# Attention scores: the queries' low part on half the rows, and one maximum per component

## The chip, the cores and the metric

The kernel runs on one core of a Trainium2 chip. The metric is device time in microseconds (us): the time of one execution, as the median of several. Names used below: PE is TensorE (matrix products), PEld its weight loads, DVE is VectorE, ACT is ScalarE, POOL is GpSimd, SP is the engine whose queue issues the loads and stores. PSUM is the memory that products are written to; it is divided into banks of 512 float32 columns.

## The reference

The layer takes 1024 latent tokens and 256 context tokens of width 1024. One projection feeds two branches, a gated linear attention and a differential attention; gates merge them, and an output projection follows. The change lies in the differential attention. It has 8 heads, and each head has two components with 64 channels:

```python
# k1, k2: 256 context keys and 1024 latent keys; q1, q2: 1024 latent queries
s1 = jnp.einsum('bhqd,bhkd->bhqk', qb1, k1).astype(jnp.float32) * scale
s2 = jnp.einsum('bhqd,bhkd->bhqk', qb2, k2).astype(jnp.float32) * scale
a = jax.nn.softmax(s1, axis=-1) - lam * jax.nn.softmax(s2, axis=-1)
return jnp.einsum('bhqk,bhkv->bhqv', a.astype(v.dtype), v)
```

Queries and keys are normalised and rotated before this. All inputs and the output are float32.

## The kernel before

**Numbers in two parts.** TensorE works on a faster float32 format of reduced precision (`fp32r` in the rows of the profile). A value is therefore split into a high and a low part, x = hi + lo, and a product of two values is made as several products of parts, summed in PSUM. For the large projections these are three (`mm3`, L331): hi x hi, hi x lo, lo x hi.

**Three phases.** Phase A makes the projections and the linear attention and stores queries, keys and values to device memory (DRAM). Phase B, about 938 to 1468 us in the profile, is the differential attention. Phase C makes the remaining branch projections and the output projection.

**Scores.** A unit is one head and 128 queries: 64 units in all. A score product contracts 64 channels, while the array has 128 rows. The rows are used for the keys' two parts: `att_keys` (L1379) loads, for each component, a tile `kk` of 128 rows and 1280 columns with the keys' high part in rows 0 to 63 and their low part in rows 64 to 127. `att_queries` (L1398) loads, for each component and each pair of query blocks, a tile `aq` with the queries' high and low part (second index 0 and 1), the same in both halves of the rows. One product with the queries' high part as weights so gives qhi x (khi + klo), and a second one with their low part adds qlo x (khi + klo). `score` in `att_scores` (L1430) issues these two for each piece of columns.

**Pieces and banks.** The scores of a unit fill five PSUM banks, the tile `s5` with 2560 columns: component 0 in columns 0 to 1279, component 1 in 1280 to 2559. Bank 2 holds the end of component 0 and the beginning of component 1, 256 columns each (`TAIL`); the other banks hold two pieces of 512 columns per component (`MAIN`). A unit has 12 products: 8 with 512 columns, 4 with 256. Three counters guard the banks: `s0` and `s1` for a component's main pieces, `st` for the shared bank. A component's counter is free again after its exponential, `st` after both.

**Softmax.** `att_max` takes a negated maximum on VectorE: one over 1024 columns for each component, and one over the shared bank for both. `att_exp` joins a component's two values with a minimum (`tensor_scalar`) and then makes the exponential of all 1280 columns on ScalarE, with the row sum as a by-product. `att_mix` joins the two components on VectorE. Then TensorE transposes the result (`att_tr`), ScalarE and GpSimd split it into parts (`split2`), and TensorE multiplies it with the values (`att_av`).

**What sets the order.** All instructions except loads and stores are put in an order by a planner (`Driver`, L57), before the program runs: tasks are generators, and each runs when what it waits for is ready by the planner's own costs (`mm` at L325 for products, `Engine` for the others); among those due, the lowest priority number goes first. On the chip each engine works through its list in that order. `yield AtPE(0)` inside a task lets other tasks place products in between. `acq` and `rel` take and give back buffers at planned times. `fill` has the last priority: its projections (24 products of 512 columns per half tile) go wherever TensorE would be free in phase B. What is left of it goes to phase C. All loads and stores go through SP's queue. `banked` (L336) declares which engine's work shares a bank with which, so that only these wait for one another.

Of the kernel before, what the change touches and what calls it, by code (L numbers as in the profile page):

```python
# [12 lines left out]
AF = mybir.ActivationFunctionType  # L13
ALU = mybir.AluOpType
AX = mybir.AxisListType
# [206 lines left out]
class Hybrid:  # L222
# [99 lines left out]
            yield  # L322
        self.d.spawn(later(), AtPE(at), prio=-9)

    def mm(self, out, lhsT, rhs, start, stop, more=False):  # L325
        self.ins = self.nc.tensor.matmul(out, lhsT, rhs, start=start, stop=stop, skip_group_check=more).ins  # L326
        n = rhs.free_size()
        c = 0.009 + max(n, 230) * 0.000428 if rhs.dtype == F32R else 0.006 + max(4 * n, 470) / 2400
        return self.d.op("PE", c, [out], [lhsT, rhs])

    def mm3(self, out, sh, sl, mh, ml, first, last, more=False):  # L331
# [1047 lines left out]
    def att_keys(self):  # L1379

        for hd in range(8):
            c, x = hd // 4, hd % 4
            for i in range(10):
                yield self.ev_st["dk", c, i]
            if hd:
                yield self.ev_q[0, 1]
            K = []
            for comp in range(2):
                rows = slice(64 * comp, 64 * comp + 64)
                yield from self.acq("kk")  # L1390
                kt = self.t("kk", [P, T], F32R)
                self.dma(kt[0:64], self.d_kT[0][c][x, rows])
                self.dma(kt[64:128], self.d_kT[1][c][x, rows])
                K.append(kt)
            self.K[hd] = K
            self.d.set(self.ev_k[hd], self.d.when(*K))

    def att_queries(self):  # L1398
        yield self.ev_b2
        for hd in range(8):  # L1400
            c, x = hd // 4, hd % 4
            for pr in range(4):
# [3 lines left out]
                for comp in range(2):  # L1406

                    src = self.d_qT[c][x, 64 * comp:64 * comp + 64, :, pr * 256:(pr + 1) * 256]
                    yield from self.acq("aq")
                    qt = self.t("aq", [P, 2, 256], F32R)  # L1410
                    for hh in range(2):
                        self.dma(qt[64 * hh:64 * hh + 64], src)
                    Q.append(qt)
                self.Q[hd, pr] = Q
                self.d.set(self.ev_q[hd, pr], self.d.when(*Q))
# [14 lines left out]
    def att_scores(self):  # L1430
# [4 lines left out]
        for hd in range(8):  # L1435
            for qt in range(8):
# [2 lines left out]
                yield self.ev_q[hd, pr]  # L1439
                K, Q = self.K[hd], self.Q[hd, pr]  # L1440

                def score(po, comp, o, n):
                    bank = po.offset % (2 * T) // 512
                    for j in range(2):
                        e = self.mm(po, Q[comp][:, j, qs], K[comp][:, o:o + n], j == 0, j == 1)
                        self.banked(self.ins, "PE", bank)
                    return e

                u = dict(hd=hd, qt=qt, E=[None, None], mt=self.t("sm", [P, 2]), mx=[self.t("sm", [P, 1]) for _ in range(2)],
                         z=self.t("sm", [P, 2]), left=2, ev=[Event() for _ in range(3)])  # L1450

                for comp in range(2):
                    yield from self.acq(f"s{comp}")
                    pm = s5[:, 1536 * comp:1536 * comp + 1024]
                    for x, (o, n) in enumerate(self.MAIN[comp]):
                        e = score(pm[:, x * 512:(x + 1) * 512], comp, o, n)
                        if x == 0:
                            yield AtPE(0)
                    d.spawn(self.att_max(u["ev"][comp], u["mx"][comp], pm, 3 * comp, 3 * comp + 1), On(e, "DVE"), prio=-3)
                    yield AtPE(0)  # L1460
                    if comp == 0:
                        yield from self.acq("st")
                        pt = s5[:, 1024:1536].rearrange("p (c k) -> p c k", c=2)
                        for x in range(2):
                            e = score(pt[:, x], x, *self.TAIL[x])
                        d.spawn(self.att_max(u["ev"][2], u["mt"], pt, 2), On(e, "DVE"), prio=-3)
                    elif qt == 7:
                        self.rel("kk", e, 2)
                    d.spawn(self.att_exp(u, comp, s5), On(e, "DVE"), prio=-3)
                    yield AtPE(0)  # L1470
                if qt % 2 == 1:
                    self.rel("aq", e, 2)
                d.set(self.ev_u[8 * hd + qt])

    def att_max(self, ev, mx, pm, *banks):
        self.dve.tensor_reduce(mx, pm, AX.X, ALU.max, negate=True)
        self.banked(self.dve.ins, "DVE", *banks)
        self.d.set(ev)
        return
        yield  # L1480

    def att_exp(self, u, comp, s5):
        d, mx = self.d, u["mx"][comp]
        yield u["ev"][2]
        yield u["ev"][comp]
        yield d.on("DVE", mx)
        self.dve.tensor_scalar(mx, mx, u["mt"][:, comp:comp + 1], None, ALU.min)
        yield from self.acq("e5")
        E = u["E"][comp] = self.t("e5", [P, T])
        yield d.on("ACT", mx)  # L1490
        e = self.act.activation(E, s5[:, 1280 * comp:1280 * comp + T], AF.Exp, bias=mx, accum_out=u["z"][:, comp:comp + 1])
        self.banked(self.act.ins, "ACT", *range(2 * comp, 2 * comp + 3))
        self.rel(f"s{comp}", e)
        u["left"] -= 1
        if u["left"] == 0:
# [19 lines left out]
        d.set(self.ev_a[u["hd"], u["qt"]], e)  # L1515


    TAIL = ((1024, 256), (0, 256))
    MAIN = (((0, 512), (512, 512)), ((256, 512), (768, 512)))
    GROUPS = ((0, 4), (4, 4), (8, 2))  # L1520

    def att_tr(self):
# [577 lines left out]
```

## Time and profile before

| | us |
|---|---|
| median of 3 executions | 1720.37 (1717.92 to 1720.63) |
| span of the profiled execution | 1714.5 |
| TensorE busy in it | 1674.2 |
| VectorE busy | 1057.7 |
| ScalarE busy | 738.3 |
| GpSimd busy | 728.8 |
| score products, TensorE busy | 180.5 |

The span runs from the first to the last instruction of one profiled execution; the profile has no other time of that execution, and the times of the other executions include what lies before and after the span. Busy times are not additive: engines work side by side. A row of a timeline gives start, length, engine, line, instruction, "output <- inputs", shape and count, and in brackets the idle time of the engine before it with what ended that. Almost all products have the same line (L326, inside `mm`), so the tiles' names tell them apart: `s<-kk,aq` are scores, `b<-ident,e` transposes, `b<-at,vv` products with the values, `mb<-h,wt` and `mc<-h,wt` projections of `fill`.

### The profile page before, as it was taken

How to read it: one execution, taken by the hardware profiler on the slowest of the kernel's cores; microseconds unless marked ns; L12 is line 12 of the kernel's file. 1: busy time of each engine (PE TensorE's matmuls, PEld its weight loads, DVE VectorE, ACT ScalarE, POOL GpSimd, SP SyncE). 2: the span in 40 equal slices, each digit the busy share in tenths (PEclk: the TensorE clock that was granted, in tenths of full speed). 3: DMA queues.
4: the chain of work that ended last, by engine and by line, in shares of the span. 5: the costliest groups of instructions: out<-in, count | busy, mean ns of one | idle time of the engine just before them, and what ended most of it. 6: DMA issues, size and time to landing. Idle time of an engine off the chain costs nothing.

```text
span 1714.5 us, 24744 instructions
## 1 busy us (share of the span) xinstructions
PE 1674.2 (98%) x8557; PEld 1389.4 (81%) x8557; DVE 1057.7 (62%) x1933; ACT 738.3 (43%) x1509; POOL 728.8 (43%) x917
## 2 busy tenths in 40 slices
PE   8899999999999999999999989999999999999999
PEld 3788788888888888888888878888888888887887
DVE  4534325615564767767763788777877778325694
ACT  4636522212242443344342566656656556311231
POOL 1500002403324445444541577878878778710000
PEclk9999999999999999999999999999999999999999
DMA  8523344453743544535444244435436753269421
GB/s 309 158 86 122 143 154 149 140 171 115 221 163 114 202 142 147 168 125 168 160 129 143 91 119 137 117 108 145 133 105 185 226 156 114 84 238 333 148 98 74
DMA packets 244748, 258.81 MB, mean 151 GB/s; under 512 B 20840, under 2 KB 176400, under 8 KB 244624
## 3 DMA queue, kind: packets, MB, share of 16 engines
q1 hardware_dynamic: 244624, 257.25, 47.7%
q8 instruction: 67, 1.10, 0.3%
q14 instruction: 57, 0.47, 0.1%
HBM read 170.68 MB, written 86.51 MB: 150 GB/s over the span
## 4 chain that ended last, share of the span: by engine, by line
PE 87%; POOL 4%; DVE 2%; DMA 2%; ACT 2%; issue 2%; SPq 0%; ACTq 0%; DVEq 0%; POOLq 0%
PE mm L326 42%; PE mc L326 11%; PE mb L326 8%; PE s L326 7%; PE b L326 5%; POOL at L190 4%; PE b L352 3%; PE go L326 3%; PE gs L326 2%; PE gt L326 2%; PE tp L352 2%; DVE sm L190 1%; PE mz L326 1%; DMA w<-in_w_ada 1%; PE gt L352 1%
## 5 line engine op out<-in xcount | busy, mean ns | idle before, releaser
L326 PE MATMUL mm<-w,h 128*128 128x512 f32 x2304 | 569.3, 399 | 1.5 <-DVE w L190 1.5
L326 PEld LDWEIGHTS mm<-w,h 128*128 128x128 f32 x2304 | 425.6, 188 | 87.6 <-DVE w L190 2.1
L190 POOL TENSOR_TENSOR at<-ac,at 128x512 fp32r<-128x512 f32 (+1 forms) x192 | 239.6, 1248 | 16.0
L190 DVE TENSOR_REDUCE sm<-s 128x1 f32<-128x1024 f32 (+1 forms) x192 | 195.7, 1039 | 55.1 <-PE s L326 47.5
L326 PE MATMUL mb<-h,wt 128*128 128x512 f32 x720 | 200.2, 410 | 1.9 <-DVE ft L190 1.1
L190 ACT ACTIVATE e<-s,sm 128x1280 f32<-128x1280 f32 x128 | 170.0, 1331 | 49.3 <-DVE sm L190 41.5
L326 PE MATMUL s<-kk,aq 128*128 128x512 f32 (+1 forms) x768 | 180.5, 367 | 10.3 <-ACT e L190 3.2
L190 POOL TENSOR_SCALAR at<-ac 128x512 fp32r<-128x512 f32 (+1 forms) x192 | 139.2, 725 | 114.2 <-ACT ac L190 108.8
L190 ACT ACTIVATE ac<-b 128x512 f32<-128x512 f32 (+1 forms) x213 | 106.8, 507 | 141.9 <-PE b L352 103.5
L190 ACT ACTIVATE p<-mm 128x512 f32<-128x512 f32 (+1 forms) x116 | 67.6, 589 | 216.9 <-PE mm L326 198.5
L326 PEld LDWEIGHTS s<-kk,aq 128*128 128x128 f32 x768 | 122.2, 190 | 32.3 <-ACT e L190 12.6
L326 PEld LDWEIGHTS mb<-h,wt 128*128 128x128 f32 x720 | 127.7, 191 | 24.4 <-DVE ft L190 1.8
L326 PE MATMUL mc<-h,wt 128*128 128x512 f32 x624 | 144.1, 390 | 0.8 <-DVE wt L190 0.5
L326 PE MATMUL mm<-h,w 128*128 128x512 f32 x576 | 142.1, 399 | 2.3 <-ACT p L190 1.4
L190 POOL TENSOR_SCALAR sm<-sm 128x1 f32<-128x1 f32 (+1 forms) x78 | 16.8, 216 | 288.6 <-DVE sm L190 166.7
L326 PEld LDWEIGHTS mc<-h,wt 128*128 128x128 f32 x624 | 116.4, 188 | 25.4 <-DVE wt L190 1.0
L326 PE MATMUL b<-at,vv 128*128 128x256 f32 x960 | 132.1, 287 | 0.3
L326 PEld LDWEIGHTS b<-at,vv 128*128 128x128 f32 x960 | 123.5, 192 | 5.2 <-ACT ac L190 1.1
L326 PEld LDWEIGHTS mm<-h,w 128*128 128x128 f32 x576 | 107.1, 189 | 25.4 <-DVE h L190 1.7
L190 DVE TENSOR_TENSOR w<-raw,w 128x512 fp32r<-128x512 f32 x120 | 86.0, 734 | 63.5 <-ACT w L190 62.4
L190 POOL TENSOR_TENSOR sm<-sm,nhalf 128x1 f32<-128x1 f32 (+2 forms) x110 | 109.6, 997 | 10.4 <-DVE sm L190 3.9
L190 DVE SCALAR_TENSOR_TENSOR e<-e,sm,e 128x1280 f32<-128x1280 f32 x64 | 113.3, 1770 | 0.8
(225 smaller groups left out, 2358.6 us busy)
## 6 DMA issues: line engine op xcount, KB each, us to landing
raw<-in_w_in SPq DMA_DIRECT2D x72, 512.0 KB, 4.3
aq<-d_qT SPq DMA_DIRECT2D x128, 128.0 KB, 3.0
d_kT<-pl SPq DMA_DIRECT2D x40, 256.0 KB, 2.3
d_dv<-pl SPq DMA_DIRECT2D x40, 256.0 KB, 2.6
kk<-d_kT SPq DMA_DIRECT2D x32, 320.0 KB, 5.3
gv<-d_v SPq DMA_DIRECT2D x40, 256.0 KB, 2.8
vv<-d_dv SPq DMA_DIRECT2D x16, 640.0 KB, 6.3
d_aT<-gpl SPq DMA_DIRECT2D x64, 128.0 KB, 2.0
```

The lines of the kernel that those rows point to most:

```text
L190: self.ins = f(out, *args, **kw).ins
L326: self.ins = self.nc.tensor.matmul(out, lhsT, rhs, start=start, stop=stop, skip_group_check=more).ins
L352: self.nc.tensor.transpose(out, src, self.ident[:n, :n])
```

## The change

- The queries' low part is multiplied with the keys' high part alone, on 64 rows; the product of the two low parts is no longer computed. A low product uses rows 0 to 63 for the first 1024 columns of component 0, and rows 64 to 127 for the other columns.
- For that, the keys lie differently: in the first 1024 columns of component 0 the high part stays in rows 0 to 63; elsewhere the two parts change places. Component 0's key tile is loaded in four pieces instead of two. Of component 1's query tile the upper half gets the high part only.
- The products of a unit come in another order: the high products of component 0's first two pieces, then a point at which other work may come in between; then, once `s1` and `st` are free, the other four high products and all six low ones without such a point. The low ones change between the halves of the rows: lower 256, upper 512, lower 256, lower 512, upper 512, lower 512 columns.
- In the shared bank the second component's high product no longer starts a sum of its own (`more`); the first component's does.
- The planner counts a low product at half its cost (`half`).
- `att_max` is gone. `att_exp` takes one maximum over all 1280 columns of its component. The maximum over the shared bank and the minima fall away. Both components' softmax tasks are started after the last product of the unit.

```diff
-    def mm(self, out, lhsT, rhs, start, stop, more=False):
+    def mm(self, out, lhsT, rhs, start, stop, more=False, half=False):
...
+        c *= 0.5 if half else 1.0
...
                 kt = self.t("kk", [P, T], F32R)
-                self.dma(kt[0:64], self.d_kT[0][c][x, rows])
-                self.dma(kt[64:128], self.d_kT[1][c][x, rows])
+                for j in range(2):
+                    for c0, n in ((0, T),) if comp else ((0, 1024), (1024, 256)):
+                        o = 64 * (j ^ (comp or c0 > 0))
+                        self.dma(kt[o:o + 64, c0:c0 + n], self.d_kT[j][c][x, rows, c0:c0 + n])
...
                     for hh in range(2):
-                        self.dma(qt[64 * hh:64 * hh + 64], src)
+                        n = 2 if hh >= comp else 1
+                        self.dma(qt[64 * hh:64 * hh + 64, :n], src[:, :n])
...
-                def score(po, comp, o, n):
-                    bank = po.offset % (2 * T) // 512
-                    for j in range(2):
-                        e = self.mm(po, Q[comp][:, j, qs], K[comp][:, o:o + n], j == 0, j == 1)
-                        self.banked(self.ins, "PE", bank)
+                def score(comp, o, lo, more=False):
+                    c0 = 1280 * comp + o
+                    n = 256 if o == self.TAIL[comp] else 512
+                    po = s5[:, c0:c0 + n]
+                    r = slice(0, P) if not lo else slice(0, 64) if c0 < 1024 else slice(64, P)
+                    e = self.mm(po, Q[comp][r, int(lo), qs], K[comp][r, o:o + n], not (lo or more), lo, True, lo)
+                    self.banked(self.ins, "PE", c0 // 512)
                     return e
...
+                yield from self.acq("s0")
+                for o in (0, 512):
+                    score(0, o, False)
+                yield AtPE(0)
+                yield from self.acq("s1")
+                yield from self.acq("st")
+                score(0, 1024, False)
+                score(1, 0, False, True)
+                for o in (256, 768):
+                    score(1, o, False)
+                for comp, o in ((0, 1024), (0, 0), (1, 0), (1, 256), (0, 512), (1, 768)):
+                    e = score(comp, o, True)
+                if qt == 7:
+                    self.rel("kk", e, 2)
                 for comp in range(2):
-                    yield from self.acq(f"s{comp}")
-                    pm = s5[:, 1536 * comp:1536 * comp + 1024]
-                    for x, (o, n) in enumerate(self.MAIN[comp]):
-                        e = score(pm[:, x * 512:(x + 1) * 512], comp, o, n)
-                        if x == 0:
-                            yield AtPE(0)
-                    d.spawn(self.att_max(u["ev"][comp], u["mx"][comp], pm, 3 * comp, 3 * comp + 1), On(e, "DVE"), prio=-3)
-                    yield AtPE(0)
-                    if comp == 0:
-                        yield from self.acq("st")
-                        pt = s5[:, 1024:1536].rearrange("p (c k) -> p c k", c=2)
-                        for x in range(2):
-                            e = score(pt[:, x], x, *self.TAIL[x])
-                        d.spawn(self.att_max(u["ev"][2], u["mt"], pt, 2), On(e, "DVE"), prio=-3)
-                    elif qt == 7:
-                        self.rel("kk", e, 2)
                     d.spawn(self.att_exp(u, comp, s5), On(e, "DVE"), prio=-3)
-                    yield AtPE(0)
+                yield AtPE(0)
...
-    def att_max(self, ev, mx, pm, *banks):
-        self.dve.tensor_reduce(mx, pm, AX.X, ALU.max, negate=True)
+    TAIL = (1024, 0)
+
+    def att_exp(self, u, comp, s5):
+        d = self.d
+        mx = u["mx"][:, comp:comp + 1]
+        sc = s5[:, 1280 * comp:1280 * comp + T]
+        banks = range(2 * comp, 2 * comp + 3)
+        self.dve.tensor_reduce(mx, sc, AX.X, ALU.max, negate=True)
         self.banked(self.dve.ins, "DVE", *banks)
...
-        yield u["ev"][2]
-        yield u["ev"][comp]
-        yield d.on("DVE", mx)
-        self.dve.tensor_scalar(mx, mx, u["mt"][:, comp:comp + 1], None, ALU.min)
         yield from self.acq("e5")
         E = u["E"][comp] = self.t("e5", [P, T])
         yield d.on("ACT", mx)
-        e = self.act.activation(E, s5[:, 1280 * comp:1280 * comp + T], AF.Exp, bias=mx, accum_out=u["z"][:, comp:comp + 1])
-        self.banked(self.act.ins, "ACT", *range(2 * comp, 2 * comp + 3))
+        e = self.act.activation(E, sc, AF.Exp, bias=mx, accum_out=u["z"][:, comp:comp + 1])
+        self.banked(self.act.ins, "ACT", *banks)
         self.rel(f"s{comp}", e)
```

More of the change, by code (lines that the diff above doesn't have):

```diff
@@ L1440, in att_scores @@
                 K, Q = self.K[hd], self.Q[hd, pr]
-                def score(po, comp, o, n):
-                    bank = po.offset % (2 * T) // 512
-                    for j in range(2):
-                        e = self.mm(po, Q[comp][:, j, qs], K[comp][:, o:o + n], j == 0, j == 1)
-                        self.banked(self.ins, "PE", bank)
-                    return e
-                u = dict(hd=hd, qt=qt, E=[None, None], mt=self.t("sm", [P, 2]), mx=[self.t("sm", [P, 1]) for _ in range(2)],
-                         z=self.t("sm", [P, 2]), left=2, ev=[Event() for _ in range(3)])
@@ new lines, in att_scores @@
+                u = dict(hd=hd, qt=qt, E=[None, None], mx=self.t("sm", [P, 2]), z=self.t("sm", [P, 2]), left=2)
+                yield from self.acq("s0")
[8 more added lines that the diff above has]
+                    score(1, o, False)
@@ L1473, in att_scores @@
                 d.set(self.ev_u[8 * hd + qt])
-    def att_max(self, ev, mx, pm, *banks):
-        self.dve.tensor_reduce(mx, pm, AX.X, ALU.max, negate=True)
-        self.banked(self.dve.ins, "DVE", *banks)
[L1478 to L1483, printed above, removed]
-        yield u["ev"][2]
-        yield u["ev"][comp]
-        yield d.on("DVE", mx)
-        self.dve.tensor_scalar(mx, mx, u["mt"][:, comp:comp + 1], None, ALU.min)
+    TAIL = (1024, 0)
[5 more added lines that the diff above has]
+        self.dve.tensor_reduce(mx, sc, AX.X, ALU.max, negate=True)
+        self.banked(self.dve.ins, "DVE", *banks)
         yield from self.acq("e5")
@@ L1515, in att_mix @@
         d.set(self.ev_a[u["hd"], u["qt"]], e)
-    TAIL = ((1024, 256), (0, 256))
-    MAIN = (((0, 512), (512, 512)), ((256, 512), (768, 512)))
     GROUPS = ((0, 4), (4, 4), (8, 2))
```

## The prediction

> **What bounds the kernel now.** I read the page first, then the stretch in which the scores are made, then the groups of that stretch, and last single products in order of time. From the page:
>
> ```profile
> span 1714.5 us, 24744 instructions
> PE 1674.2 (98%) x8557; PEld 1389.4 (81%) x8557; DVE 1057.7 (62%) x1933; ACT 738.3 (43%) x1509; POOL 728.8 (43%) x917
> PEclk9999999999999999999999999999999999999999
> PE 87%; POOL 4%; DVE 2%; DMA 2%; ACT 2%; issue 2%; SPq 0%; ACTq 0%; DVEq 0%; POOLq 0%
> ```
>
> TensorE is busy for 98% of the span at full clock, and the chain of waits is 87% TensorE. The stretch with the scores, all engines and then the score tile alone:
>
> ```profile
> 938.00:1468.00 530.00, 508.68 (x3053) 434.95 (x3054) 409.04 (x730) 320.64 (x647) 412.08 (x442) 0.99 0.47 136
> 938.00:1468.00 530.00, 180.49 (x768) 122.17 (x768) 195.69 (x192) 179.28 (x256) 0.99 0.47 136
> ```
>
> The columns are length, then PE, PEld, DVE, ACT and POOL busy (the second row has no POOL). TensorE is free for only 21.3 of 530 us, with the other engines busy for 60 to 78%. Scores are a third of its work; most of the rest are AV products, transposes and projections of `fill`, whose priority is the lowest and which take every gap. A stretch that runs slower is filled with them, so what counts is TensorE's own time per unit (one head, 128 queries) and the waits that `fill` cannot cover.
>
> **Prices of a product.** Products are pipelined: a row's length less one product's own duration is the spacing of the others.
>
> ```profile
> 1548.50 97.10 PE mc L326 x427
> 1129.46 1.60 PE L326 MATMUL b<-at,vv 128*128 128x256 f32 x12
> 1126.95 0.60 PE L352 MATMUL b<-ident,e 128*128 128x128 f32 x4
> ...
> L326 PE MATMUL s<-kk,aq 128*128 128x512 f32 x512 | 146.4, 403 | 6.1 <-ACT e L190 2.7 <-DVE b1k L190 2.7 <-ACT p L190 0.7
> L326 PE MATMUL s<-kk,aq 128*128 128x256 f32 x256 | 44.1, 293 | 4.2 <-DMA kk<-d_kT 2.8 <-ACT e L190 0.5 <-issue 0.4
> L352 PE MATMUL b<-ident,e 128*128 128x128 f32 x604 | 94.2, 276 | 7.3 <-ACT ac L190 6.1 <-DVE b1k L190 1.2
> ```
>
> A product of 512 columns takes 97.10/427 = 0.227 us. One of 256 takes (1.60 - 0.29)/11 = 0.119. One of 128 takes (0.60 - 0.276)/3 = 0.108, hardly less than 256, so I read 0.108 as what one weight load needs when loads follow each other.
>
> A unit has twelve score products, 8 of 512 and 4 of 256 columns; half of them are the low pass. It costs 4 x 0.227 + 2 x 0.119 = 1.146 us, or 73.3 us over 64 units. Nothing more than a part of this can be gained.
>
> **The low pass on half the rows.** The high pass stays as it is. The low products have the same columns but 64 rows, in the order lower 256, upper 512, lower 256, lower 512, upper 512, lower 512 ("upper" is rows 0 to 63). The trace has no pair of products on different rows, so I bound it. If the halves run side by side without friction, the lower half's line decides: 2 x 0.119 + 2 x 0.227 = 0.692 us. If not at all, it stays at 1.146. In between, each of the six still needs its own load of 128 columns. With loads 0.108 apart and each waiting until the product before it on its half has begun, the six begin at 0, 0.108, 0.216, 0.335, 0.432 and 0.562, and the last ends at 0.789. I take 0.789, because the 128-column row shows that loads in sequence are not free: a gain of 0.357 us per unit, 22.8 us in all, with 0 and 29.1 as the ends.
>
> The Trainium skill ("TensorE: Matmul & The Clock Gate", Measured speedup vs the span model) has packed products starting about 4 ns apart and lasting hardly longer than one. That would put the low pass at the frictionless end; no row here shows it.
>
> **Two changes of the array's shape per unit.** A unit now goes from 128-row products to 64-row ones and back. The trace has two changes like it: from 2-row transposes to 128-row ones, and from 128 output columns to 2.
>
> ```profile
> 23.73 0.40 PE L352 MATMUL gt<-ident,p 2*128 2x2 f32 x4 [0.44 <-DVE p L190]
> 23.93 0.20 PE L352 MATMUL gt<-ident,p 2*128 2x2 f32 x1
> 24.06 0.44 PE L352 MATMUL tp<-ident,g 128*128 128x128 f32 x2
> ...
> 33.02 0.63 PE L326 MATMUL mm<-h,w 128*128 128x512 f32 x2
> 33.49 0.40 PE L326 MATMUL gs<-pl,cs 128*2 128x512 f32 x1
> 1106.46 0.75 PE L326 MATMUL s<-kk,aq 128*128 128x256 f32 x4
> ```
>
> The 2-row products follow each other by (0.40 - 0.20)/3 = 0.067. The first 128-row one comes 0.13 after the last of them, 0.063 late, with no wait noted. Its successor comes 0.44 - 0.27 = 0.17 later (0.27 is what a transpose product lasts, 276 ns in the row above) instead of 0.108: the load was not done ahead, another 0.06. That makes 0.12 for a change of rows. With score weights the uncovered load costs more: the 256-column row gives 0.75 - 0.29 = 0.46 for three spacings against 3 x 0.119, so 0.10, and the change would cost 0.063 + 0.10 = 0.16. The change of output columns shows nothing: 0.47 from the first row's start for two spacings of 0.227. The ends are therefore 0 and, if the array empties wholly (a 512-column product lasts 0.403, 0.176 beyond its spacing) before a load of 0.10 begins, 0.28. I take 0.14, the middle of 0.12 and 0.16, since a change of rows is the nearer row: 0.28 per unit, 17.9 us over 128 changes, with 0 and 36 as the ends.
>
> The Trainium skill ("TensorEngine Tiling (Array Packing)", Key Properties) says that changing the tiling mode, not just the tile, drains TensorE. This speaks against the change. The 2-row rows agree (0.12), the 2-column rows do not (0). By the rule every unit pays twice, as in my sum; by the column row it pays nothing, which is the first rival.
>
> **Maxima.** Per component one maximum over 1280 columns replaces one over 1024, half of a shared one over 2 x 256, and the minimum that joined them.
>
> ```profile
> L190 DVE TENSOR_REDUCE sm<-s 128x1 f32<-128x1024 f32 x128 | 155.9, 1218 | 54.0 <-PE s L326 46.5 <-ACT ac L190 2.6 <-ACT e L190 2.5
> L190 DVE TENSOR_REDUCE sm<-s 128x2 f32<-128x512 f32 x64 | 43.6, 682 | 1.0 <-PE s L326 1.0
> L190 DVE TENSOR_SCALAR sm<-sm,sm 128x1 f32<-128x1 f32 x186 | 32.6, 207 | 1.3
> ```
>
> The slope (1218 - 682)/512 gives 1.05 ns per column, so 1280 columns take 1.49 us; 128 of them are 190 us against 155.9 + 43.6 = 199.5. The 128 minima, at 0.207, save 26 us. VectorE is relieved by 36 us, 0.56 per unit. I count this as nothing, because VectorE has 121 us free in the stretch and `fill` covers what TensorE would wait for it; at best it takes away part of the waits below.
>
> **Order and loads.** Before, a unit's products come in four pieces with room for other work between; now two products come first and ten follow at once, behind a wait for both exponentials of the previous unit. Queued behind that wait are transposes, AV and `fill`, and behind the transposes ScalarE's copies and GpSimd's subtractions. Today's waits and loads there:
>
> ```profile
> PEld s L326 <- ACT e L190: 12.6, 20, 2.9
> PE s L326 <- ACT e L190: 3.2, 7, 0.9
> PE s L326 <- DMA kk<-d_kT: 2.8, 1, 2.8
> kk<-d_kT SPq DMA_DIRECT2D x32, 320.0 KB, 5.3
> aq<-d_qT SPq DMA_DIRECT2D x128, 128.0 KB, 3.0
> ```
>
> Two key loads per head become four smaller ones: 16 more issues on SP's queue, in 530 us. Each pair of query blocks loads 64 KB less. Keys come free at the same product (the last one of a head's eighth unit), and the component loaded last keeps its two loads, so I count the loads as nothing; without the cover of other TensorE work a late key costs what it cost once, 2.8 us.
>
> **Sum.** Low pass -22.8, changes of shape +17.9, the rest 0: -4.9 us on the profiled span of 1714.5. That span is 5.9 below the median of 1720.37, and I carry the difference over: 1715.5.
>
> **Rivals.**
> *A, the changes of shape are free* as with output columns: -22.8 to -29.1, so 1691 to 1698. For it: the 2-column rows, and weight loads that are otherwise done ahead. Against it: the 2-row rows.
>
> *B, my forecast*: a low pass of 0.69 to 0.79 and changes at 0.12 to 0.16 gain 0.037 to 0.214 us per unit: 1707 to 1718, and about 3 more each way for waits.
>
> *C, it doesn't do what it says*: 64-row products follow one another like others. Then the low pass stays at 1.146 and only the changes remain: 1738 at 0.14 each, 1756 at the upper end, 1720 if they are free. For it: no overlap of two products in the trace. Against it: the products share neither rows nor banks.
>
> *D, slower because TensorE waits at the head of its queue* for the previous unit's second exponential. The place is the wait before the ten products. In some units the first maximum now runs between the pieces:
>
> ```profile
> 1145.53 1.07 PE L326 MATMUL s<-kk,aq 128*128 128x512 f32 x4
> 1146.71 1.23 DVE L190 TENSOR_REDUCE sm<-s 128x1 f32<-128x1024 f32 x1 [0.36 <-PE s L326]
> 1150.18 1.57 PE L326 MATMUL s<-kk,aq 128*128 128x256 f32 x8
> 1151.87 1.81 DVE L190 TENSOR_REDUCE sm<-s 128x2 f32<-128x512 f32 x2
> 1153.60 0.33 DVE L190 TENSOR_SCALAR sm<-sm 128x1 f32<-128x1 f32 x2
> 1153.84 0.33 DVE L190 TENSOR_SCALAR sm<-sm,sm 128x1 f32<-128x1 f32 x2
> 1154.28 1.34 ACT L190 ACTIVATE e<-s,sm 128x1280 f32<-128x1280 f32 x1
> ```
>
> Here 1.81 + 0.33 of maxima and minima follow the last product; afterwards it would be 2 x 1.49 = 2.98 before the second exponential, 0.84 later. The price: if each of 64 units waits the 0.63 that one wait has now (12.6/20), that is 40 us in place of 15.8, so +24 on my sum: 1740. It decides from about 0.3 us per unit of waiting that the written order didn't foresee. Against it: the first exponential no longer waits for three maxima, and the order is planned with these durations.
>
> **Chances.** B 0.40, A 0.28, C 0.16, D 0.14, others 0.02. I treat 0.2% (3.4 us) as the limit of what a measurement tells from no change. Of B, 0.22 is faster than that, 0.14 within it, 0.04 slower; of C, 0.04 is within. Faster: 0.28 + 0.22 = 0.50; within: 0.18; slower: 0.04 + 0.12 + 0.14 + 0.02 = 0.32. The range must reach both A and the nearer ends of C and D: 1690 to 1740. B's own is 1704 to 1721.
>
> **What would show it.** Low products on the two halves start closer than 0.227 (about 0.11 apart); at their normal spacing C holds. The first low product and the first product after the last show an extra 0.12 to 0.16; if nothing, A. The score tile's TensorE busy time should fall from 180.5 by some 5 us under B and 25 under A. The waits for ACT e should stay near 16 us; near 40 is D. VectorE's stretch should be lighter by 36 us with 128 maxima of about 1.49. The forecast is wrong if a change of shape costs under 0.05 or over 0.25, or if the two halves don't overlap.

## The result and the profile after

The changed kernel takes 1765.33 us (median of 4 executions, 1764.33 to 1767.2). The kernel before took 1719.23 beside it (1717.92 to 1720.63). The ratio is 1.0274, with a 95% interval of 1.0259 to 1.0289: 46 us slower. That is outside the range of the prediction, which had forecast a kernel slightly faster. From the page of the changed kernel:

```profile
span 1762.6 us, 24561 instructions
PE 1684.3 (96%) x8557; PEld 1363.7 (77%) x8557; DVE 1031.5 (59%) x1741; ACT 733.6 (42%) x1509; POOL 741.6 (42%) x917
PE   8899999999999999999999999999998998969999
PEclk9999999999999999999999999999999999989999
PE 82%; POOL 4%; issue 4%; DVE 4%; DMA 3%; ACT 3%; SPq 1%; ACTq 0%; DVEq 0%; POOLq 0%
L190 DVE TENSOR_REDUCE sm<-s 128x1 f32<-128x1280 f32 x128 | 184.8, 1485 | 58.2 <-PE s L326 58.0
L190 ACT ACTIVATE e<-s,sm 128x1280 f32<-128x1280 f32 x128 | 170.2, 1332 | 107.4 <-DVE sm L190 107.3
```

The span grew by 48.1 us (1714.5 to 1762.6). TensorE's busy time accounts for 10.1 of it (1674.2 to 1684.3), its idle time for 38.0 (40.3 to 78.3). VectorE's 128 maxima last 1.485 us each, as forecast; it is lighter by 26 us over the span, where the forecast had 36 for the stretch. The last row shows the new thing: ScalarE stands idle for 107.4 us before the exponentials, 107.3 of them waiting for maxima. The same row of the page before has less than half of that:

```profile
L190 ACT ACTIVATE e<-s,sm 128x1280 f32<-128x1280 f32 x128 | 170.0, 1331 | 49.3 <-DVE sm L190 41.5
```

Busy times by stretch (length, then PE, PEld, DVE, ACT and POOL, granted clock, DMA share, GB/s); the second row is the score tile alone:

```profile
938.00:1541.00 603.00, 563.58 (x3258) 445.58 (x3256) 391.56 (x545) 316.66 (x640) 415.67 (x431) 0.98 0.47 136
938.00:1541.00 603.00, 157.17 (x768) 95.36 (x768) 181.94 (x126) 177.43 (x252) 0.98 0.47 136
1550.00:1600.00 50.00, 34.30 (x202) 30.46 (x201) 10.02 (x28) 13.48 (x37) 33.63 (x43) 0.86 0.33 109
1600.00:1762.00 162.00, 154.82 (x671) 127.27 (x670) 110.88 (x170) 39.05 (x62) 0.00 (x0) 0.98 0.41 140
```

TensorE is free for 39.4 us of the score stretch, and for 15.7 of the 50 us from 1550. TensorE's groups by shape (busy time, mean ns, idle time before them) show what filled the rest:

```profile
L326 PE MATMUL mb<-h,wt 128*128 128x512 f32 x960 | 259.6, 409 | 4.0 <-DVE ft L190 2.7 <-DVE wt L190 0.5 <-ACT ft L190 0.5
L326 PE MATMUL mc<-h,wt 128*128 128x512 f32 x384 | 90.7, 398 | 4.2 <-DMA h<-d_bT 4.2
L326 PE MATMUL s<-kk,aq 128*128 128x512 f32 x256 | 84.3, 411 | 18.5 <-ACT e L190 17.8 <-ACT p L190 0.7
L326 PE MATMUL s<-kk,aq 64*128 64x512 f32 x256 | 62.5, 423 | 0.0
L326 PE MATMUL s<-kk,aq 64*128 64x256 f32 x128 | 32.4, 333 | 0.0
L326 PE MATMUL s<-kk,aq 128*128 128x256 f32 x128 | 28.3, 302 | 4.1 <-ACT e L190 2.6 <-issue 1.0 <-DMA aq<-d_qT 0.6
```

The `fill` products inside phase B (`mb`) rose from 720 to 960; those left for later (`mc`) fell from 624 to 384. So the stretch swallowed 240 more of them, 54 us at 0.227 each, and after that TensorE waited all the same. Waits of the whole span (us in total, times, longest):

```profile
ACT e L190 <- DVE sm L190: 107.3, 51, 5.7
DVE sm L190 <- ACT e L190: 91.8, 47, 5.0
PEld s L326 <- ACT e L190: 29.0, 27, 2.5
PE s L326 <- ACT e L190: 20.3, 22, 2.3
```

The three engines wait for each other in a ring: scores for exponentials (49.3 us; 15.8 before), exponentials for maxima, maxima for the next scores. One unit of it, in order of time:

```profile
1133.98 2.23 PE L326 MATMUL s<-kk,aq 128*128 128x512 f32 x12
1136.02 2.89 DVE L190 TENSOR_REDUCE sm<-s 128x1 f32<-128x1280 f32 x2 [1.90 <-PE s L326]
1138.94 1.33 ACT L190 ACTIVATE e<-s,sm 128x1280 f32<-128x1280 f32 x1 [1.43 <-DVE sm L190]
1140.41 0.73 PE L326 MATMUL s<-kk,aq 128*128 128x512 f32 x2 [1.24 <-ACT e L190]
1140.53 1.33 ACT L190 ACTIVATE e<-s,sm 128x1280 f32<-128x1280 f32 x1
1142.00 1.87 PE L326 MATMUL s<-kk,aq 128*128 128x256 f32 x10 [0.41 <-ACT e L190]
```

All twelve products first, then both maxima (2.89), and only after the second maximum the first exponential (1136.02 + 2.89 = 1138.91, start 1138.94). The next unit's ten products follow the second exponential (1140.53 + 1.33 = 1141.86, start 1142.00). The first exponential does not need the second maximum's value. Both read bank 2: component 0 lies in banks 0 to 2, component 1 in banks 2 to 4, and `banked` makes ScalarE's read of a shared bank wait for VectorE's. The planner places both maxima ahead, so that wait is for the second one.

### The profile page after: what moved, and what is told of

The parts are those of the page before. It is cut to its first block, busy times and chain, and to the rows that moved or that the text cites. A ratio compares the mean times of both kernels' runs of the same rounds, so it can differ in the third digit from the quotient of the medians.

```text
span 1762.6 us, 24561 instructions
## 1 busy us (share of the span) xinstructions
PE 1684.3 (96%) x8557; PEld 1363.7 (77%) x8557; DVE 1031.5 (59%) x1741; ACT 733.6 (42%) x1509; POOL 741.6 (42%) x917
## 4 chain that ended last, share of the span: by engine, by line
PE 82%; POOL 4%; issue 4%; DVE 4%; DMA 3%; ACT 3%; SPq 1%; ACTq 0%; DVEq 0%; POOLq 0%
PE mm L326 41%; PE mb L326 11%; PE mc L326 7%; PE s L326 6%; PE b L326 4%; POOL at L190 3%; PE b L353 3%; PE go L326 3%; DVE sm L190 2%; PE gs L326 2%; PE gt L326 2%; PE tp L353 2%; DMA w<-in_w_ada 1%; ACT e L190 1%; PE mz L326 1%
## 5 line engine op out<-in xcount | busy, mean ns | idle before, releaser
L326 PE MATMUL mb<-h,wt 128*128 128x512 f32 x960 | 259.6, 409 | 4.0 <-DVE ft L190 2.7
L190 POOL TENSOR_TENSOR at<-ac,at 128x512 fp32r<-128x512 f32 (+1 forms) x192 | 245.6, 1279 | 16.0
L190 POOL TENSOR_SCALAR at<-ac 128x512 fp32r<-128x512 f32 (+1 forms) x192 | 143.0, 745 | 181.1 <-ACT ac L190 173.1
L190 DVE TENSOR_REDUCE sm<-s 128x1 f32<-128x1280 f32 x128 | 184.8, 1485 | 58.2 <-PE s L326 58.0
L190 ACT ACTIVATE e<-s,sm 128x1280 f32<-128x1280 f32 x128 | 170.2, 1332 | 107.4 <-DVE sm L190 107.3
L326 PEld LDWEIGHTS mb<-h,wt 128*128 128x128 f32 x960 | 173.1, 192 | 39.4 <-DVE ft L190 4.4
L326 PE MATMUL s<-kk,aq 128*128 128x512 f32 (+3 forms) x768 | 157.2, 384 | 22.6 <-ACT e L190 20.3
L326 PEld LDWEIGHTS s<-kk,aq 128*128 128x128 f32 (+1 forms) x768 | 95.4, 191 | 61.9 <-ACT e L190 29.0
L190 POOL TENSOR_TENSOR sm<-sm,nhalf 128x1 f32<-128x1 f32 (+2 forms) x110 | 115.0, 1045 | 8.8 <-DVE sm L190 2.0
L353 PE MATMUL b<-ident,e 128*128 128x128 f32 x600 | 97.1, 279 | 12.8 <-DVE b1k L190 8.2
L353 PEld LDWEIGHTS b<-ident,e 128*128 128x128 f32 x600 | 71.1, 141 | 39.9 <-DVE b1k L190 10.3
```

The source lines that it names most:

```text
L190: self.ins = f(out, *args, **kw).ins
L353: self.nc.tensor.transpose(out, src, self.ident[:n, :n])
```

## Experiments

Two explanations stand against each other. **The ring**: softmax starts later in a unit and the first exponential waits for both maxima, so the ring per unit became longer than TensorE's own work. **TensorE's side**: the products themselves, their changes of shape, or the batch of ten without a gap. Where an expectation names theories by letters, P is the batch of ten products and the one it is set against is the ring. Beside both stands the question of whether `fill` simply ran out. Differences in microseconds are against the kernel before on the same chip (1715.72, 1716.89 and 1718.32 in the three sets; the change's own +46.1 is against 1719.23). Lines of an edit that are not shown are marked with three dots.

**full128: the low products on all 128 rows**, keys and queries laid out as before, order and maxima as in the change.

```diff
...
-    r = slice(0, P) if not lo else slice(0, 64) if c0 < 1024 else slice(64, P)
-    e = self.mm(po, Q[comp][r, int(lo), qs], K[comp][r, o:o + n], not (lo or more), lo, True, lo)
+    e = self.mm(po, Q[comp][:, int(lo), qs], K[comp][:, o:o + n], not (lo or more), lo, True)
```

> The changed kernel's order and maxima, but the low products on all 128 rows, with the keys and queries laid out as before. Theory R (ring): a unit's scores wait for the exponentials of the unit before, and the steps products, two maxima in sequence, two exponentials follow one another; this took 8.24 us per unit before and 9.47 us after, 79 us more over 64 units than fill's spare 55 us can cover. By R the rows are not to blame: 9.5 to 9.7 us per unit and 1760 to 1775 us. Theory S (shape): the changes between 128 and 64 rows and the 64-row products cost the time; by S it is back at 1715 to 1725 us.

Measured: 1768.23, ratio 1.0300 (1.0276 to 1.0325), +52.5 us. So the loss is there without any product on half the rows, and with the same waits:

```profile
ACT e L190 <- DVE sm L190: 99.4, 49, 5.4
PEld s L326 <- ACT e L190: 34.7, 34, 2.8
PE s L326 <- ACT e L190: 22.7, 31, 2.6
```

That clears the changes of shape; the half rows, with all that belongs to them, are worth 6 us beside it, and the two intervals overlap.

**onemax: the kernel before with one maximum per component**, and nothing else of the change.

```diff
-    d.spawn(self.att_max(u["ev"][comp], u["mx"][comp], pm, 3 * comp, 3 * comp + 1), On(e, "DVE"), prio=-3)
...
-    d.spawn(self.att_max(u["ev"][2], u["mt"], pt, 2), On(e, "DVE"), prio=-3)
...
...
-        self.dve.tensor_scalar(mx, mx, u["mt"][:, comp:comp + 1], None, ALU.min)
+        self.dve.tensor_reduce(mx, s5[:, 1280 * comp:1280 * comp + T], AX.X, ALU.max, negate=True)
+        self.banked(self.dve.ins, "DVE", *range(2 * comp, 2 * comp + 3))
```

> The kernel before, with only the maxima changed: one of 1280 columns per component in place of three and two minima; products, rows and their order as before. Ring theory R: the first maximum starts after the shared bank's products instead of 1.8 us before the last product, but the minima fall away; the sum of the steps is about 8.2 us per unit, as before, and the time 1712 to 1730 us. If the maxima alone make the loss: above 1745 us.

Measured: 1733.80, ratio 1.0109 (1.0093 to 1.0124), +18.1: dearer than expected. VectorE does 31 us less than before (1026.5 against 1057.7), and the kernel is slower for it. Its waits show the ring without any of the new products:

```profile
ACT e L190 <- DVE sm L190: 100.8, 54, 4.9
PEld s L326 <- ACT e L190: 39.1, 59, 3.0
PE s L326 <- ACT e L190: 20.5, 23, 2.6
```

**tailfirst: the changed kernel with its maxima cut differently.** Component 1's 256 columns of bank 2 come first, then component 0's 1280, then component 1's other 1024, and a minimum joins component 1's two. Now the last read of bank 2 on VectorE is that of component 0, and the first exponential need not wait for the second component. It costs VectorE 64 maxima and 64 minima more than the change.

```diff
...
-        self.dve.tensor_reduce(mx, sc, AX.X, ALU.max, negate=True)
-        self.banked(self.dve.ins, "DVE", *banks)
+        if comp == 0:
+            self.dve.tensor_reduce(mt, s5[:, T:T + 256], AX.X, ALU.max, negate=True)
+            self.banked(self.dve.ins, "DVE", 2)
+            self.dve.tensor_reduce(mx, sc, AX.X, ALU.max, negate=True)
+            self.banked(self.dve.ins, "DVE", *banks)
+        else:
+            self.dve.tensor_reduce(mx, sc[:, 256:], AX.X, ALU.max, negate=True)
+            self.banked(self.dve.ins, "DVE", 3, 4)
+            yield d.on("DVE", mx)
+            self.dve.tensor_scalar(mx, mx, mt, None, ALU.min)
```

> The changed kernel, but the maximum of component 1's 256 columns in the shared bank is taken first, then component 0's, then the other 1024 columns of component 1, joined by a minimum; so the first exponential no longer has to wait for the second component's maximum. Ring theory R: from the last product to the end of the second exponential 6.67 us become about 5.0, a unit takes about 8.0 us, fill no longer runs out, and the time is 1708 to 1722 us. Rival P (the ten products issued without a gap hold up transposes and AV products): the order of products is unchanged, so it stays above 1750 us.

Measured: 1708.88, ratio 0.9963 (0.9953 to 0.9973), -6.8. This one edit gives back 53 us (+46.1 to -6.8) although VectorE works 16 us more. Its page, its waits and one unit:

```profile
span 1705.6 us, 24637 instructions
PE 1667.0 (98%) x8557; PEld 1354.7 (79%) x8557; DVE 1047.8 (61%) x1869; ACT 736.1 (43%) x1509; POOL 732.2 (43%) x917
```

```profile
ACT e L190 <- DVE sm L190: 59.9, 36, 4.3
PEld s L326 <- ACT e L190: 8.1, 11, 1.7
```

```profile
1105.81 1.76 PE L326 MATMUL s<-kk,aq 128*128 128x256 f32 x10
1107.14 2.96 DVE L190 TENSOR_REDUCE sm<-s 128x1 f32<-128x256 f32 x3 [1.09 <-PE s L326]
1109.00 1.33 ACT L190 ACTIVATE e<-s,sm 128x1280 f32<-128x1280 f32 x1
1110.13 0.21 DVE L190 TENSOR_SCALAR sm<-sm,sm 128x1 f32<-128x1 f32 x1
1110.38 1.33 ACT L190 ACTIVATE e<-s,sm 128x1280 f32<-128x1280 f32 x1
```

The three maxima take as long as the two did (2.96 against 2.89), but the first exponential starts at 1109.00, 1.10 before they end, and the second follows at once. The time is as the ring explanation expected; the steps are less so: from the last product's start to the second exponential's end it is 5.69 us and not 5.0, and a unit takes 8.49 us and not 8.0.

**morefill: eight more half tiles of work for `fill`** in the changed kernel, taken out of phase A, to see whether `fill` ran out.

```diff
-        NM = 1
+        NM = 0
```

> The changed kernel, but four tiles of projections (8 half tiles, about 44 us of TensorE) go from phase A to fill in phase B; the sum of the work is the same. Ring theory R: the loss comes where fill has run out (about 16 us idle from 1550 to 1600 us, and half-clock stretches there), so 15 to 30 us come back: 1732 to 1750 us. If the loss is TensorE's own work in the scores or waits that fill can't cover, it stays at 1760 us or more.

Measured: 1772.63, ratio 1.0332 (1.0316 to 1.0347), +56.9: it was expected to help if work were lacking, and it is 11 us slower than the change. Its windows, for the score stretch and the 50 us behind it, and the projections left over:

```profile
923.00:1536.00 613.00, 574.39 (x3305) 455.85 (x3306) 390.77 (x540) 320.35 (x647) 417.64 (x434) 0.98 0.44 128
1536.00:1586.00 50.00, 50.00 (x307) 43.95 (x304) 16.00 (x36) 16.73 (x40) 35.99 (x42) 1.00 0.51 172
```

```profile
L326 PE MATMUL mc<-h,wt 128*128 128x512 f32 x528 | 126.4, 394 | 2.4 <-DMA h<-d_bT 1.6 <-DVE wt L190 0.5 <-ACT wt L190 0.2
```

528 - 384 = 144 of the movable products are left, and the hole after the scores is gone (50.00 of 50 us busy). Inside the stretch TensorE is still free for 38.6 us. So the gaps there do not come from a lack of work. The total time says less, because the edit opened another hole where the work was taken out, ahead of the scores. The same window of the change and of this run:

```profile
870.00:923.00 53.00, 53.00 (x270) 45.02 (x269) 26.30 (x68) 21.98 (x62) 17.62 (x39) 1.00 0.40 119
870.00:923.00 53.00, 32.74 (x143) 25.50 (x141) 27.18 (x62) 18.20 (x54) 16.92 (x40) 0.83 0.26 81
```

It stands empty for 20.3 us there, more than the 15.7 that it filled behind the scores. By single instructions of the trace, 37.9 of the 39.4 idle us of the change lie between the last product of one half tile of `fill` and the first of the next. `fill` has one PSUM bank, which must be emptied in between (mean gap 5.5 us, 40 half tiles); 30.5 of the 37.9 us pass before the instruction that empties it has ended. Whether a second bank would close these gaps was not tried: all eight banks are in use.

**yields: points for other work inside the batch of ten.** In the changed kernel other tasks may place products after each of the second component's three high products.

```diff
                 score(1, 0, False, True)
+                yield AtPE(0)
                 for o in (256, 768):
                     score(1, o, False)
+                    yield AtPE(0)
```

> The changed kernel, but other tasks may place products after each of the three last high pieces; the low products stay together. Ring theory R: nothing is gained, since what follows the last product is unchanged; 1758 to 1785 us. Rival P (the uninterrupted ten products hold up other work): 1745 us or less.

Measured: 1784.79, ratio 1.0392 (1.0376 to 1.0409), +67.9. If the long batch were the cause, breaking it up would have helped. Instead the ring grows by 0.30 us per unit (9.47 to 9.77 on average): 0.10 between a unit's third and last product, 0.20 from a second exponential to the next unit's third product. That costs 22 us more.

**threemax: the changed kernel's products with the kernel before's maxima** (1024, shared bank, 1024, two minima), all started after the last product.

```diff
...
+                pt = s5[:, 1024:1536].rearrange("p (c k) -> p c k", c=2)
+                for ev, mx, pm, banks in ((0, u["mx"][0], s5[:, :1024], (0, 1)), (2, u["mt"], pt, (2,)),
+                                          (1, u["mx"][1], s5[:, 1536:], (3, 4))):
+                    d.spawn(self.att_max(u["ev"][ev], mx, pm, *banks), On(e, "DVE"), prio=-3)
...
```

> The changed kernel's products, rows and order, but with the three maxima and two minima of the kernel before, all behind the last product: the first exponential then reads banks 0 to 2 while no maximum that it shares a bank with is under way, but VectorE still takes all three maxima before the first minimum. Ring theory R: the maxima take 1.22 + 0.68 + 1.22 + 2 x 0.21 = 3.5 us instead of 2.97, and the first exponential waits for all of them by VectorE's order, so nothing or little is gained: 9.2 to 10 us per unit, 1745 to 1785 us. If the single maximum per component as such were the whole loss: 1725 us or less.

Measured: 1738.24, ratio 1.0109 (1.0092 to 1.0126), +19.9, below what was expected. So the order and rows of the products, with all maxima started behind the last of them, cost some 20 us with the old maxima; the new maxima cost some 18 with the old products, and both 46: 8 more than the sum. It also shows that the length of the softmax alone does not set the time: here it is the longest of all (6.97 us in the table below), yet the next unit's last product starts 2.14 us after the second exponential's end instead of 2.86 in the change, and the profiled execution has 60.6 us of idle time instead of 78.3 and a clock of 0.999 instead of 0.986. What makes these differ was not traced.

**oldorder_tf: the kernel before's products, order and rows with tailfirst's maxima.**

```diff
...
-        self.dve.tensor_reduce(mx, s5[:, 1280 * comp:1280 * comp + T], AX.X, ALU.max, negate=True)
-        self.banked(self.dve.ins, "DVE", *range(2 * comp, 2 * comp + 3))
+        if comp == 0:
+            self.dve.tensor_reduce(mt, s5[:, T:T + 256], AX.X, ALU.max, negate=True)
+            self.banked(self.dve.ins, "DVE", 2)
+            self.dve.tensor_reduce(mx, s5[:, :T], AX.X, ALU.max, negate=True)
+            self.banked(self.dve.ins, "DVE", 0, 1, 2)
+        else:
+            self.dve.tensor_reduce(mx, s5[:, T + 256:], AX.X, ALU.max, negate=True)
+            self.banked(self.dve.ins, "DVE", 3, 4)
+            yield d.on("DVE", mx)
+            self.dve.tensor_scalar(mx, mx, mt, None, ALU.min)
```

(The lines taken out are those of onemax; against the kernel before, the edit takes out what onemax takes out.)

> The kernel before (products and their order, all 128 rows), with tailfirst's maxima: after the shared bank's products its 256 columns of component 1, then component 0's 1280, and after component 1's main products its 1024 and one minimum. Against onemax (1733.8 us) only the wait of the first exponential for the second maximum is gone. If that wait is the loss of onemax: 1708 to 1722 us. If the first maximum's later start (it began 1.8 us before the last product in the kernel before) is: 1725 us or more.

Measured: 1705.18, ratio 0.9929 (0.9913 to 0.9945), -11.7: below what was expected and the fastest of all, ahead of both kernels of this change. Against onemax the freed first exponential is worth 29.8 us here. On average its first maximum starts together with the last product, as in onemax and 1.8 us later than in the kernel before; so a late first maximum alone is not the loss. Its waits:

```profile
ACT e L190 <- DVE sm L190: 43.6, 37, 4.0
PEld s L326 <- ACT e L190: 6.2, 12, 1.1
```

**minfirst: the kernel before, with one wait shortened.** There the first component's minimum could stand behind the second component's maximum on VectorE; on average the first exponential started 0.23 us after the last maximum's end. Here it is issued right after the shared bank's maximum.

```diff
...
     def att_max(self, ev, mx, pm, *banks, u=None):
         self.dve.tensor_reduce(mx, pm, AX.X, ALU.max, negate=True)
         self.banked(self.dve.ins, "DVE", *banks)
+        if u:
+            yield u["ev"][0]
+            self.dve.tensor_scalar(u["mx"][0], u["mx"][0], mx[:, 0:1], None, ALU.min)
...
```

> The kernel before with one thing changed: component 0's minimum is taken right after the shared bank's maximum, ahead of component 1's main maximum, so that the first exponential doesn't wait for the latter (0.2 us behind all maxima in the kernel before). The wait that made the loss in the changed kernel is then a smaller one in the kernel before too. By R the ring gets shorter by up to 1 us per unit, fill covers better, and the time is 1700 to 1714 us; if TensorE's own work is the only bound there, no change (1713 to 1720 us).

Measured: 1713.57, ratio 0.9975 (0.996 to 0.999), -4.8. The time lies in both ranges of the expectation, so it doesn't decide between them; the gain of 4.8 is clear of its interval, and an earlier first exponential gains a little even where the ring hardly bound.

**nopair: tailfirst with all low products on the lower half**, so that no two run on different rows.

```diff
...
-    r = slice(0, P) if not lo else slice(0, 64) if c0 < 1024 else slice(64, P)
+    r = slice(0, P) if not lo else slice(64, P)
```

> As tailfirst with the same order of instructions, but all low products use the lower 64 rows, so no two can run side by side; the keys' high part lies in rows 64 to 127 throughout. If the halves run side by side in tailfirst, its low pass of 0.692 us becomes 1.146: 0.45 us per unit, 29 us in all, so 1732 to 1745 us. If the halves gain nothing: 1706 to 1714 us.

Measured: 1738.63, ratio 1.0127 (1.0111 to 1.0143), +21.7: 28.5 us above tailfirst. Score tile alone, tailfirst and then nopair:

```profile
938.00:1476.00 538.00, 157.76 (x765) 93.01 (x765) 186.13 (x189) 178.32 (x252) 0.99 0.47 136
```

```profile
938.00:1505.00 567.00, 187.86 (x759) 116.87 (x760) 190.96 (x189) 178.43 (x252) 0.98 0.44 127
```

187.86 - 157.76 = 30.1 us more on TensorE, nearly all of which arrives in the time: with its waits gone, this kernel is bound by TensorE.

**tailfirst128: tailfirst with the low products on all 128 rows** (full128's edit on it).

```diff
...
-    e = self.mm(po, Q[comp][r, int(lo), qs], K[comp][r, o:o + n], not (lo or more), lo, True, lo)
+    e = self.mm(po, Q[comp][:, int(lo), qs], K[comp][:, o:o + n], not (lo or more), lo, True)
```

> As tailfirst (shared bank's maximum first, order of products of the changed kernel), but the low products on all 128 rows as in the kernel before. It prices the 64 rows alone where the ring is short: the changed kernel's trace gives 0.327 us from the last high product to the first low one, 0.574 to the last low one and 0.324 to the next product, 1.225 us, to which some 0.08 us of a load done late come, against 0.227 + 1.146 = 1.373 us on 128 rows. So TensorE loses 0.07 us per unit, 4 to 5 us: 1712 to 1718 us if TensorE's work is the bound. If the ring is still the bound, the 0.15 us by which the products end later count too: up to 1728 us.

Measured: 1733.22, ratio 1.0094 (1.0076 to 1.0112), +16.3: 23 us above tailfirst, more than expected. Its six low products and their neighbours take only some 0.1 us per unit more (next section), 7 us in all. The planner also sees other costs and plans another order. Its page, beside tailfirst's above:

```profile
span 1731.1 us, 24634 instructions
PE 1681.8 (97%) x8557; PEld 1392.9 (80%) x8557; DVE 1058.7 (61%) x1869; ACT 734.8 (42%) x1509; POOL 738.7 (43%) x917
```

Of the 25.5 us between the two spans, 10.7 are idle time of TensorE (38.6 to 49.3). From the granted clock (0.995 to 0.991), an estimated 1731.1 x 0.009 - 1705.6 x 0.005 = 7 are slower work. With the 7 us of products that is nearly all of it. Why this plan leaves more idle time and a lower clock was not traced.

The ring by single instructions, as means over the 64 units in us (first columns) beside the measured difference:

| kernel | first product to next unit's | last product's start to the second exponential's end | difference in time |
|---|---|---|---|
| before | 8.24 | 5.84 | 0 |
| oldorder_tf | 8.20 | 5.77 | -11.7 |
| tailfirst | 8.49 | 5.69 | -6.8 |
| tailfirst128 | 8.78 | 5.81 | +16.3 |
| nopair | 8.93 | 5.59 | +21.7 |
| onemax | 8.66 | 6.51 | +18.1 |
| threemax | 9.09 | 6.97 | +19.9 |
| after | 9.47 | 6.67 | +46.1 |
| full128 | 9.40 | 6.33 | +52.5 |

The four kernels with the late first exponential or the late maxima have the long second column; the four with tailfirst's maxima have the short one, whatever their products. The column does not order the times by itself: nopair has a short one and loses by TensorE's work, and tailfirst's unit is longer than that of the kernel before, with a shorter time.

## Why the prediction was wrong, point by point

**Low pass and changes of shape: the sum was near, by errors that cancel.** One unit of the changed kernel, each row from a narrower window of the timeline:

```profile
1124.75 1.30 PE L326 MATMUL s<-kk,aq 128*128 128x512 f32 x7
1125.08 0.97 PE L326 MATMUL s<-kk,aq 64*128 64x256 f32 x6
1125.98 0.33 PE L353 MATMUL b<-ident,b1k 128*128 128x128 f32 x1
```

The last high product starts at 1124.75, the first low one 0.33 later instead of 0.227: 0.10 late. The six low ones take 0.97 in all; less the last one's own 0.40 their starts span 0.57. The next full-height product follows at 1125.98, 0.33 after the last low start: again 0.10 late. Medians over the 64 units are 0.327, 0.574 and 0.324. In full128, with the same order on all rows, they are 0.233, 0.930 and 0.231, and the product after that comes 0.108 later against 0.165 in the change. Together 1.502 and 1.390: a gain of 0.11 us per unit, 7 us in all, where the forecast had 0.077 and 4.9.

The low pass as a whole (0.574 + 0.227 = 0.80) is close to the 0.789 I took, but that is luck. I had the six starts at 0, 0.108, 0.216, 0.335, 0.432 and 0.562; their medians are 0, 0.003, 0.223, 0.341, 0.343 and 0.574. The halves run side by side without friction, and one start is late: the lower half's second product comes 0.223 after its first, a product of 256 columns, against 0.116 in full128. nopair has the same 0.223 before its second product and full128's spacings behind it. There the load of this product starts 0.107 after the first product, while the later loads start 2 to 3 ns after the product before them. So this is a load that was not done ahead, behind the change of shape. Booked there, the two changes cost 0.094 + 0.107 + 0.093 + 0.057 = 0.35 us per unit against 0.28 forecast, and the low pass gains 1.146 - 0.692 = 0.454 against 0.357. The rule that I weighed against the change, from the Trainium skill ("TensorEngine Tiling (Array Packing)", Key Properties: a change of tiling mode drains TensorE), agrees in that each change delays the next product by 0.10 us; it gives no size.

**Rivals A and C fall.** A needed free changes of shape. C needed products that do not run side by side: nopair is that kernel, and it is 28.5 us slower, where C's lost overlap was priced at 22.8. The pairs on different halves start 3 ns apart (1125.081 and 1125.084 in the unit above).

**My sign for A and B was a bad one.** I expected the score tile's busy time to fall by 5 us under B and 25 under A. It fell by 23.3 (180.49 to 157.17), though B's terms are what happened. A row's busy time ends with its last product's own end. The 0.10 us by which the next tile's product is late lies inside that end and does not show in it, and a unit in two pieces has fewer such ends than one in four (in full128, with the same pieces on all rows, the tile is busy for some 176). Spacings of single products tell it; busy times of a tile do not.

**The loads: right.** The groups of DMA issues give the key loads 4.2 to 4.8 us from issue to landing, and the score products of the change waited for no load but 0.6 us for queries (the last of the groups above).

**Maxima "as nothing": the step that failed.** The sum put maxima, order and loads at 0. My reason was that VectorE has time to spare "and `fill` covers what TensorE would wait for". VectorE's load indeed fell, by 26 us, and its spare time was of no use: what changed was not how much it does but when its results come. Before, a unit's first maximum ran between the pieces of its products; on average it started 1.8 us before the last product did. In the change it starts 0.33 after it, so that both long maxima lie behind the last product. The last of them ends 3.22 us after that product's start instead of 2.27, and the second exponential 6.67 instead of 5.84. These 0.83 us per unit are the 0.84 that I worked out under rival D; the sum counted them as nothing. Another 0.42 us come from the new order: the ten products stand behind the second exponential, and the last of them starts 2.86 us after its end instead of 2.44. And the first exponential stands behind the second component's maximum, which I did not see: the two share bank 2. It stood behind all maxima in the kernel before as well, where the first maximum was done early; here this wait is what tailfirst takes away, and the time with it. I even wrote, against rival D, that "the first exponential no longer waits for three maxima". It waited for two that lasted 2.89 together. The Trainium skill ("PSUM — Partial Sum Buffer", PSUM bank collisions raise a hardware error) says that two engines must not touch the same partitions of one bank at once, two reads included. No run here let them; the kernel's declared waits keep them apart, and tailfirst therefore changes the order and removes no wait.

**"Filled with them" was the premise under it.** I took the gaps as free because the projections of `fill` "take every gap". A unit became 1.23 us longer (8.24 to 9.47), 79 us over 64 units. `fill` took 54 us of this by running 240 products earlier. The rest stayed idle, because its one bank lets it run only part of the time, and when it was used up another 15.7 us of the 50 after 1550 stood empty. It delays a loss; it did not cover it. morefill shows that more of it closes the hole behind the scores and not the gaps inside them (38.6 us).

**Rival D named the place and missed the size.** It put the loss at the wait before the ten products, and its sign (waits for ACT e near 40 us) came true at 49.3. It priced only those waits: 1740. Not in that price were the empty stretch after `fill` ran out and TensorE's clock: 0.986 over the span against 0.995. That is an estimated 1762.6 x 0.014 - 1714.5 x 0.005 = 16 us, rather too high because part of the slow clock fell on idle time. With 38.0 us more idle time it leaves 6 us less of own work in the 48.1, near the 7 above. I gave D 0.14 because VectorE seemed relieved; the order of its reads was the thing to look at.

What stays open: why the plan of tailfirst128 leaves more idle time, what makes threemax faster than the change in spite of its longer softmax, and why the clock falls. Low-clock stretches come with idle ones in the change (0.86 in the stretch from 1550), but threemax has 39.6 us of idle time in its score stretch at a clock of 0.999.

## What to carry to other kernels

When an engine has spare time, ask when its results come rather than how much it does: once the ring (products, maximum, exponential, next products) is longer than the bound engine's own work in it, only filler covers the difference. Before merging two reductions, list which banks each reader touches; a tile that shares a bank makes the first consumer wait for the last reader, and cutting that bank's reduction out and placing it first was worth 53 us here and 30 in the old order. Low-priority filler counts as cover only for as long as it lasts and as often as its own buffer is free.

## What the runs showed of the hardware

- Products on the two halves of the rows start 3 ns apart. The Trainium skill ("TensorE: Matmul & The Clock Gate", Measured speedup vs the span model) gives about 4 ns, and this case's trace agrees. I had taken loads in sequence, 0.108 apart.
- The six starts still span 0.57 us, not the 0.465 of a frictionless lower half (0.119 + 0.119 + 0.227): the lower half's second product comes 0.22 after its first, which has only 256 columns. Its load starts 0.107 after the first product's start; in full128 each load starts 3 ns after the product before it.
- Products of 64 rows on one half alone follow one another like those of 128 rows, except right after the change of shape: the five spacings are 0.223, 0.231, 0.118, 0.233 and 0.236 us in nopair (medians), and 0.116, 0.231, 0.117, 0.233 and 0.236 in full128. The whole difference between 1.039 and 0.930 us lies in the first.
